# Hybrid attention encoder on one core: one wide buffer per chunk of keys, values or queries, and the copy of a group's sums moved behind the exponentials

## The chip, the cores and the metric

The kernel runs on one core of a Trainium2 chip. The core has TensorE (PE, the matrix engine), VectorE (DVE), ScalarE (ACT), GpSimd (POOL) and SyncE (SP), which here only issues transfers. Each engine works through its own instructions in order. The metric is the device time of one execution in microseconds (us); lower is better.

## The reference, cut to what matters

One encoder layer is computed for a prompt of 256 tokens and a sample of 2048 tokens, apart from each other:

```python
h    = rmsnorm(x, norm_pre)                       # 1024 wide
u, b, c, z_conv, q_lat, kv_lat, k_pe, z_attn = split(h @ w_in)
conv = b * short_conv(c * u, conv_w) * silu(z_conv)       # 3 taps, 512 wide
q    = rmsnorm(q_lat, q_norm) @ w_uq              # 384 -> 8 heads x (64 + 32)
kv   = rmsnorm(kv_lat, kv_norm) @ w_ukv           # 256 -> 8 heads x (64 keys + 64 values)
q    = [q_nope, rope(q_pe)];  k = [k_nope, rope(k_pe) for every head]
att  = softmax(q @ k.T / sqrt(96)) @ v * silu(z_attn)     # full, not causal
y    = x + rmsnorm([conv, att] @ w_out, norm_post)
```

Everything is float32. The kernel keeps that precision by splitting values into a high and a low part and multiplying the parts apart: three matmuls (lines 91 to 93) for one product.

## The kernel before

**Phase 1** (up to about 646 us) makes the combined projection. It leaves the latents, the gates and the convolution branch in DRAM.

**Phase 2** turns the latents into keys, values and queries, chunk by chunk. There are nine chunks of 256 tokens, one of the prompt and eight of the sample. Keys and values of all chunks come first (`keys`: four products `m`, each 128 rows by 256 tokens; `values`: two products of 128 tokens by 512), then the queries in the order 1, 2, 0, 3, ..., 8 (`queries`: six products; `m` 4 and 5, which come first, are the parts to be rotated, 0 to 3 the rest). A product takes its PSUM buffer from `bank`, which goes in a cycle of three: the first half of a wide buffer (128 x 1024), its second half, and a narrow buffer "o" (128 x 512). There are two wide and two narrow "o" buffers. The halves of a wide buffer are one tile for the program that places the waits, which has this visible effect in the trace: a matmul into the second half waits for the reads of the first.

Each product of keys or queries is read at once by `split` (line 71: ScalarE writes the high part `sk` or `sq`; line 72: VectorE the low part), or by `rope` (lines 578 to 581: VectorE a shuffle and a product, GpSimd a product and a sum). The rotated queries `sqr` are split into `sqp` at `m == 2`, and `sqp` is stored in DRAM there; `sq` is stored at `m == 3`. `sqr` and `sqp` exist once each, blocks `sk` and `sq` have three buffers together. SyncE's transfers stand in one queue, in an order that the scheduler of the language gives them; the order on TensorE, VectorE, ScalarE and GpSimd is that in which the program is written, from the first key block on.

Once the keys are in DRAM, the heads' keys are loaded (`k`, line 688 ff.), eight transfers that use the hardware's queue of SyncE, and the queries of block 0 after the chunks 1 and 2 (`load_q(0)`, line 714), since block 0 is 512 queries of the sample's first two chunks. From the third query chunk of the sample on, the generator `beside` goes on by two pieces for each query product: the first maxima of block 0 (`m`, line 751; VectorE's reduction `mx`, line 752; two narrow buffers "m"), then the prompt's whole attention.

**Phase 3, attention** (832 to 1531 us) has 16 groups, one for each pair of heads and block of 512 queries, with eight periods each. A period takes two tiles of 128 keys. Its score matmuls go into two wide buffers (`first`, line 788: two matmuls for each head and tile; `second`, line 793: one with the maxima). Between the first ones stand the maxima of a group to come, after the second ones the products with the values for the period before (line 917, into a narrow buffer "o"). Then ScalarE takes the two exponentials (line 798, 128 x 1024 each, into `p`) and GpSimd adds each `p` to the running sum `acc` (line 808). The sums of a group are used in the next one. `finish` begins there at the third period (`at == 2`): two matmuls add `acc` over the partitions (`r`, line 817, a buffer "m"), ScalarE copies `r` to `rsum` (line 819), VectorE takes four reciprocals (line 822), GpSimd multiplies the gate with them (line 824), VectorE multiplies the result with the gate (`res`, line 827) and frees the buffer "o" by it. Each call of `settle` goes one `yield` further, one call to a period, and in the period it stands ahead of the exponentials:

```python
self.settle()
for x, o in enumerate(os):
    s = 2 * p + x
    self.exponents(s, o)
    if at or x:
        self.total(n, ...)
```

While the groups 0 to 13 run, the output weights are cut in pieces by ScalarE and GpSimd (`spare`).

**Phase 4** multiplies 18 tiles of 128 tokens with the output weights, in the order 16, 17, 0, ..., 15. A tile is split as well: ScalarE writes the high part (line 942), GpSimd the low part (line 943), and the last eight of 24 matmuls for each half of the output (line 956) use the low part. The split of the first tile (16) is written after the last period.

Of the kernel before, what the change touches and what calls it, by code (L numbers as in the profile page):

```python
# [21 lines left out]
P = 128  # L22
# [37 lines left out]
def f(ap):  # L60
    return ap.bitcast(F32)
# [327 lines left out]
class Phase2:  # L389
# [169 lines left out]
    def run(self, pv):  # L559
# [3 lines left out]
        with ExitStack() as ctx:  # L563
            pb = ctx.enter_context(tc.tile_pool(name="p2b", bufs=2, reuse_waits="tile"))

            def bank(name):
                self.turn += 1
                if self.turn % 3 == 0:
                    return g.narrow(name, "o")
                if self.turn % 3 == 1:  # L570
                    self.pair = g.wide(name)
                half = self.turn % 3 - 1
                return self.pair[:, half * 512 : (half + 1) * 512]

# [14 lines left out]

            def keys(ci):  # L590
# [3 lines left out]
                hi, lo = ws["uk"]  # L594
                for m in range(4):
                    o = bank(f"k{ci}_{m}")[:, :n]
                    msl = slice(m * P, (m + 1) * P)
                    mm3(nc, o, [(hi[:, k, msl], lo[:, k, msl], lt[:, :, 0, k], lt[:, :, 1, k]) for k in range(2)])
                    split(nc, sk[:, 0, m], sk[:, 1, m], o, BACK)
                    if m == 3:  # L600
                        store(g.kn, sk, slice(at, at + n))
                    yield "k", ci, m

            def values(ci):
                at, n = self.chunks[ci]
                lt, _ = self.lt["kv", ci]
                hi, lo = ws["uv"]
                for m in range(n // P):
                    o = bank(f"v{ci}_{m}")
                    mm3(nc, o, [(lt[:, m, 0, k], lt[:, m, 1, k], hi[:, k, :], lo[:, k, :]) for k in range(2)])  # L610
                    nc.scalar.activation(pv[:, at // P + m], o, AF.Copy, scale=BACK)
                    yield "v", ci, m

            def queries(ci):
# [6 lines left out]
                hi, lo = ws["uq"]  # L621
                for m in (4, 5, 0, 1, 2, 3):
                    o = bank(f"q{ci}_{m}")[:, :n]
                    msl = slice(m * P, (m + 1) * P)
                    mm3(nc, o, [(hi[:, k, msl], lo[:, k, msl], lt[:, :, 0, k], lt[:, :, 1, k]) for k in range(3)])
# [524 lines left out]
```

## Time and profile before

| what | time |
| --- | --- |
| median of three runs | 1751.0 us (1750.26 to 1751.06) |
| the profiled execution | 1750.81 us |
| its span in the profile | 1748.9 us |
| TensorE busy (matmuls) | 1658.3 us, 95% |
| GpSimd busy | 859.4 us, 49% |
| VectorE busy | 757.9 us, 43% |
| ScalarE busy | 591.0 us, 34% |
| mean granted clock of TensorE | 0.990 |
| GpSimd's running sum `acc`, one of 224 | 2.354 us |
| GpSimd's product of gate and `rsum`, one of 16 | 1.27 us |

The span is the time between the first and the last instruction in the trace. TensorE is nearly always busy, so the pauses that remain on it, and the stretches in which its clock falls, are what a change of order can alter; a busy share of another engine tells only whether it could take more work. The granted clock is given as a share of full speed.

### The profile page before, as it was taken

The numbers are of one execution on the slowest core, as the hardware profiler recorded it, in microseconds if no ns is written. First come the engines' busy times: TensorE is split into PE (matmuls) and PEld (weight loads), VectorE is DVE, ScalarE is ACT, GpSimd is POOL, SyncE is SP. The second block draws the span as 40 slices with busy tenths as digits, with TensorE's granted clock in tenths as the row PEclk, the third lists the DMA queues.
The fourth block names the chain that finished last, engine by engine and source line by source line (L and its number), as shares of the span: only waits on it lengthen the run. The fifth ranks groups of instructions, "written<-read, shape, count | busy, mean of one in ns | idle before, by whom it ended". The sixth has DMA issues, their size and how long they took to land.

```text
span 1748.9 us, 22522 instructions
## 1 busy us (share of the span) xinstructions
PE 1658.3 (95%) x8870; PEld 1120.3 (64%) x8870; DVE 757.9 (43%) x1214; ACT 591.0 (34%) x867; POOL 859.4 (49%) x638
## 2 busy tenths in 40 slices
PE   8999999999999997787999999999999999989998
PEld 8999999999999984555333333333333333368886
DVE  4333332323663312365555555555655555122222
ACT  7521112452231123322444444444444444511111
POOL 3221221122522110123788888889888888942222
PEclk9999999999999999988999999999999999999999
DMA  8921112544342124646111131113111210034443
GB/s 285 284 75 49 58 51 88 147 122 122 102 141 81 64 75 119 169 140 162 38 30 31 43 85 36 43 31 91 30 43 31 67 43 13 13 108 144 139 133 114
DMA packets 141741, 158.97 MB, mean 91 GB/s; under 512 B 33842, under 2 KB 118116, under 8 KB 141636
## 3 DMA queue, kind: packets, MB, share of 16 engines
q1 hardware_dynamic: 141636, 157.55, 30.1%
q8 instruction: 69, 1.13, 0.3%
q14 instruction: 36, 0.29, 0.1%
HBM read 109.72 MB, written 41.89 MB: 87 GB/s over the span
## 4 chain that ended last, share of the span: by engine, by line
PE 48%; ACT 2%; DVE 2%; issue 1%; POOL 1%; POOLq 0%; ACTq 0%; DVEq 0%
PE o L917 13%; PE s L788 12%; PE out L954 7%; PE m L751 6%; PE out L956 4%; PE s L793 4%; POOL acc L808 1%; ACT p L798 1%; DVE mx L752 1%; PE r L817 1%; PE mr L775 1%; ACT rsum L819 1%; PE q L91 0%; PE q L93 0%; PE q L92 0%
## 5 line engine op out<-in xcount | busy, mean ns | idle before, releaser
L808 POOL TENSOR_TENSOR acc<-acc,p 128x1024 f32<-128x1024 f32 x224 | 527.3, 2354 | 81.7 <-ACT p L798 68.8
L752 DVE TENSOR_REDUCE mx<-m 128x1 f32<-128x512 f32 x512 | 338.6, 691 | 270.8 <-PE m L751 270.8
L798 ACT ACTIVATE p<-s,exps 128x1024 f32<-128x1024 f32 x256 | 271.3, 1112 | 300.3 <-PE s L793 295.9
L788 PE MATMUL s<-q,k 128*128 128x512 f16 x1024 | 301.5, 379 | 26.5 <-ACT p L798 26.5
L91 PE MATMUL o<-hdn_hi,whi 128*128 128x384 f32 x960 | 323.5, 337 | 0.0
L92 PE MATMUL o<-hdn_lo,whi 128*128 128x384 f32 x960 | 322.7, 336 | 0.0
L93 PE MATMUL o<-hdn_hi,wlo 128*128 128x384 f32 x960 | 322.6, 336 | 0.0
L917 PE MATMUL o<-p,v 128*64 128x512 f32 x1024 | 247.7, 605 | 0.0
L788 PEld LDWEIGHTS <-k 128*128 128x128 f16 x1024 | 91.7, 98 | 211.5 <-issue 120.6
L751 PE MATMUL m<-k,q 96*128 96x512 f16 x512 | 194.5, 381 | 2.3 <-DVE mx L752 1.5
L91 PEld LDWEIGHTS o<-hdn_hi,whi 128*128 128x128 f32 x960 | 180.5, 188 | 0.5
L92 PEld LDWEIGHTS o<-hdn_lo,whi 128*128 128x128 f32 x960 | 180.5, 188 | 0.0
L93 PEld LDWEIGHTS o<-hdn_hi,wlo 128*128 128x128 f32 x960 | 180.5, 188 | 0.0
L917 PEld LDWEIGHTS o<-p,v 128*64 128x64 f32 x1024 | 62.2, 136 | 127.5 <-issue 127.0
L954 PE MATMUL out<-wo,o_cut 128*128 128x512 f32 x576 | 140.4, 396 | 0.0
L954 PEld LDWEIGHTS out<-wo,o_cut 128*128 128x128 f32 x576 | 108.0, 188 | 27.6 <-ACT o_cut L942 0.8
L943 POOL TENSOR_TENSOR o_cut<-o_raw,o_cut 128x1024 fp32r<-128x1024 f32 x18 | 43.0, 2393 | 118.6 <-ACT o_cut L942 118.6
L236 ACT ACTIVATE whi<-w 128x1024 fp32r<-128x1024 f32 x40 | 42.2, 1058 | 172.0 <-PE o L92 157.8
L279 POOL TENSOR_TENSOR gt<-gt,z 128x384 f32<-128x384 f32 x24 | 29.4, 1224 | 142.0 <-ACT z L278 142.0
L962 DVE TENSOR_TENSOR yt<-out,g_post 128x1024 f32<-128x1024 f32 x18 | 22.1, 1225 | 163.6 <-ACT junko L961 163.6
L751 PEld LDWEIGHTS <-q 96*128 96x128 f16 x512 | 49.4, 96 | 59.3 <-issue 1.3
L271 POOL TENSOR_TENSOR cu<-cu,rb 128x384 f32<-128x384 f32 (+2 forms) x28 | 27.5, 987 | 112.5 <-DVE cu L270 112.5
(229 smaller groups left out, 2030.9 us busy)
## 6 DMA issues: line engine op xcount, KB each, us to landing
w<-in_w_e_dram SPq DMA_DIRECT2D x40, 512.0 KB, 3.4
x<-in_x_dram SPq DMA_DIRECT2D x18, 512.0 KB, 6.2
o_raw<-mix_s SPq DMA_DIRECT2D x18, 512.0 KB, 4.7
o_raw<-in_x_dram SPq DMA_DIRECT2D x18, 512.0 KB, 5.6
out_dram<-yt SPq DMA_DIRECT2D x18, 512.0 KB, 6.2
q<-qn_s SPq DMA_DIRECT2D x64, 128.0 KB, 2.8
xt<-in_x_t_dram SPq DMA_DIRECT2D x5, 1536.0 KB, 8.2
k<-kn_s SPq DMA_DIRECT2D x12, 512.0 KB, 6.2
```

The costliest lines, as they stand in the source:

```text
L91: nc.tensor.matmul(out, sh, mh, start=first and i == 0, stop=False)
L92: nc.tensor.matmul(out, sh, ml, start=False, stop=False)
L93: nc.tensor.matmul(out, sl, mh, start=False, stop=last and i == n - 1)
L751: nc.tensor.matmul(m, q[:DQK, i, 2, b * P : (b + 1) * P], k[:DQK, i, 1, c * 512 : (c + 1) * 512], start=True, stop=True)
L752: nc.vector.reduce_max(mx[:, u, c : c + 1], m, axis=AX.X)
L788: nc.tensor.matmul(o, k[:, ki, x, ks], q[:, qi, x, :], start=x == 0, stop=False)
L793: self.g.nc.tensor.matmul(o, self.kc[rows, ks], c[rows], start=False, stop=True)
L798: nc.scalar.activation(p, o, AF.Exp, scale=g.exps[:, 0:1])
L808: nc.gpsimd.tensor_tensor(self.acc[key], self.acc[key], first, op=ALU.add)
L917: nc.tensor.matmul(self.o[n][i * DV : (i + 1) * DV], g.v[:, kt, h * DV : (h + 1) * DV], p[:, i * QB : (i + 1) * QB], start=kt == 0, stop=k ...
L954: nc.tensor.matmul(o[:, w], mh[:, k, :], wk[k // 2][:, k % 2, w], start=k == 0 and wk is hi, stop=False)
L956: nc.tensor.matmul(o[:, w], ml[:, k, :], hi[k // 2][:, k % 2, w], start=False, stop=k == 7)
```

## The change

It has three edits. In phase 2, `bank` goes; the four products of a key chunk, the two of a value chunk and the four unrotated ones of a query chunk fill one wide buffer of their own (`wide`), and it is read once, when whole: one `split` over 1024 columns, or one copy. The two rotated products share one narrow buffer and one `rope` over 512 columns. The split and store of `sqp` stand after those of `sq`, at `m == 3`. In attention, `settle` stands behind the loop over the two exponentials and sums. In phase 4, the low part of the first tile (16) is made by VectorE instead of GpSimd.

```diff
@@ -563,21 +563,13 @@ Phase2.run
-            def bank(name):
-                self.turn += 1
-                if self.turn % 3 == 0:
-                    return g.narrow(name, "o")
-                if self.turn % 3 == 1:
-                    self.pair = g.wide(name)
-                half = self.turn % 3 - 1
-                return self.pair[:, half * 512 : (half + 1) * 512]
-
-            def rope(dst, src, tb, n, name):
-
-                t = pb.tile([P, CB], F32, tag="rs", bufs=2, name=f"rs_{name}")[:, :n]
+            def rope(dst, src, tb, name):
+
+                t = pb.tile([P, 2, CB], F32, tag="rs", bufs=2, name=f"rs_{name}")[:, :, : src.shape[2]]
+                cos, sin = (tb[:, w : w + 1, : src.shape[2]].to_broadcast(list(src.shape)) for w in range(2))
                 nc.vector.stream_shuffle(t, src, SWAP)
-                nc.vector.tensor_tensor(dst, src, tb[:, 0, :n], op=ALU.mult)
-                nc.gpsimd.tensor_tensor(t, t, tb[:, 1, :n], op=ALU.mult)
+                nc.vector.tensor_tensor(dst, src, cos, op=ALU.mult)
+                nc.gpsimd.tensor_tensor(t, t, sin, op=ALU.mult)
                 nc.gpsimd.tensor_tensor(dst, dst, t, op=ALU.add)
...
+            def wide(name, m, n):
+                return g.wide(name)[:, : m * n].rearrange("p (m t) -> p m t", m=m)
 
             def keys(ci):
...
+                o = wide(f"k{ci}", 4, n)
                 for m in range(4):
-                    o = bank(f"k{ci}_{m}")[:, :n]
                     msl = slice(m * P, (m + 1) * P)
...
-                    split(nc, sk[:, 0, m], sk[:, 1, m], o, BACK)
                     if m == 3:
+                        split(nc, sk[:, 0], sk[:, 1], o, BACK)
                         store(g.kn, sk, slice(at, at + n))
                     yield "k", ci, m
...
+                o = wide(f"v{ci}", n // P, H * DV)
                 for m in range(n // P):
-                    o = bank(f"v{ci}_{m}")
...
-                    nc.scalar.activation(pv[:, at // P + m], o, AF.Copy, scale=BACK)
+                    if m == n // P - 1:
+                        nc.scalar.activation(pv[:, at // P : (at + n) // P], o, AF.Copy, scale=BACK)
                     yield "v", ci, m
...
+                r = g.narrow(f"qr{ci}", "o")[:, : 2 * n].rearrange("p (m t) -> p m t", m=2)
+                o = wide(f"q{ci}", 4, n)
                 for m in (4, 5, 0, 1, 2, 3):
-                    o = bank(f"q{ci}_{m}")[:, :n]
                     msl = slice(m * P, (m + 1) * P)
...
-                    if m >= 4:
-                        rope(sqr[:, m - 4], o, tb, n, f"q{ci}_{m}")
-                    else:
-                        split(nc, sq[:, 0, m], sq[:, 1, m], o, BACK)
-                    if m == 2:
+                    if m == 5:
+                        rope(sqr, r, tb, f"q{ci}")
+                    if m == 3:
+                        split(nc, sq[:, 0], sq[:, 1], o, BACK)
+                        store(g.qn, sq, tok)
                         split(nc, sqp[:, 0], sqp[:, 1], sqr, BACK)
                         store(g.qr, sqp, tok)
-                    if m == 3:
-                        store(g.qn, sq, tok)
                     yield "q", ci, m
@@ -894,12 +889,12 @@ Attention.steps
-        self.settle()
         for x, o in enumerate(os):
             s = 2 * p + x
             self.exponents(s, o)
             if at or x:
                 self.total(n, self.p[s - 1] if not at else self.p[s], None if at else self.p[s])
+        self.settle()
@@ -940,7 +935,9 @@ Phase4.split
         m, _, mh, ml = self.ready[i]
         nc.scalar.activation(mh, m, AF.Copy)
-        nc.gpsimd.tensor_tensor(ml, m, f(mh), op=ALU.subtract)
+
+        eng = nc.vector if i == T // P - 2 else nc.gpsimd
+        eng.tensor_tensor(ml, m, f(mh), op=ALU.subtract)
```

ScalarE's order in attention, around the third period of the second group; `s` are score tiles, `p` their exponentials, `r` the partition sums. Before:

```order
L798 ACTIVATE p_7795<-s_7765,exps 128x1024
L798 ACTIVATE p_7797<-s_7766,exps 128x1024
L798 ACTIVATE p_7833<-s_7802,exps 128x1024
L798 ACTIVATE p_7836<-s_7803,exps 128x1024
L819 ACTIVATE rsum_7873<-r_7870 128x512
L798 ACTIVATE p_7875<-s_7840,exps 128x1024
L798 ACTIVATE p_7878<-s_7841,exps 128x1024
```

After (line numbers are those of the changed kernel, in which 793 is the exponential and 814 the copy):

```order
L793 ACTIVATE p_7635<-s_7604,exps 128x1024
L793 ACTIVATE p_7638<-s_7605,exps 128x1024
L793 ACTIVATE p_7672<-s_7642,exps 128x1024
L793 ACTIVATE p_7675<-s_7643,exps 128x1024
L814 ACTIVATE rsum_7681<-r_7678 128x512
L793 ACTIVATE p_7713<-s_7683,exps 128x1024
L793 ACTIVATE p_7716<-s_7684,exps 128x1024
```

The copy has moved from ahead of the third period's two exponentials to behind them.

GpSimd's order at the end of the same `finish`, in the group's seventh period; `gate` is the product of line 824 before, 819 after, all others are running sums. Before:

```order
L808 TENSOR_TENSOR acc_7799<-acc_7799,p_7986 128x1024
L808 TENSOR_TENSOR acc_7799<-acc_7799,p_7989 128x1024
L824 TENSOR_TENSOR gate_7427<-gate_7427,rsum_7873 128x512
L808 TENSOR_TENSOR acc_7799<-acc_7799,p_8027 128x1024
L808 TENSOR_TENSOR acc_7799<-acc_7799,p_8030 128x1024
L808 TENSOR_TENSOR acc_7799<-acc_7799,p_8079 128x1024
```

After:

```order
L803 TENSOR_TENSOR acc_7601<-acc_7601,p_7787 128x1024
L803 TENSOR_TENSOR acc_7601<-acc_7601,p_7790 128x1024
L803 TENSOR_TENSOR acc_7601<-acc_7601,p_7827 128x1024
L803 TENSOR_TENSOR acc_7601<-acc_7601,p_7830 128x1024
L819 TENSOR_TENSOR gate_7229<-gate_7229,rsum_7681 128x512
L803 TENSOR_TENSOR acc_7601<-acc_7601,p_7878 128x1024
```

The product with the gate stands two sums later than it did against the exponentials' tiles: it was ahead of the seventh period's sums, and is now behind them.

VectorE's order in the first query chunk of phase 2: the rotation (a shuffle and a product), the splits `sq`, and the split `sqp` of the rotated part. Before:

```order
L578 STREAM_SHUFFLE rs_q_4_6290<-q_4_6280 128x256
L579 TENSOR_TENSOR sqr_6277<-q_4_6280,tb_6147 128x256
L578 STREAM_SHUFFLE rs_q_5_6304<-q_4_6280 128x256
L579 TENSOR_TENSOR sqr_6277<-q_4_6280,tb_6147 128x256
L72 SCALAR_TENSOR_TENSOR sq_6279<-q_0_6309,sq_6279 128x256
L72 SCALAR_TENSOR_TENSOR sq_6279<-q_1_6321,sq_6279 128x256 x2
L72 SCALAR_TENSOR_TENSOR sqp_6278<-sqr_6277,sqp_6278 128x512
L72 SCALAR_TENSOR_TENSOR sq_6279<-q_3_6347,sq_6279 128x256
```

After:

```order
L570 STREAM_SHUFFLE rs_q_6219<-qr_6199 128x512
L571 TENSOR_TENSOR sqr_6196<-qr_6199,tb_6084 128x512
L72 SCALAR_TENSOR_TENSOR sq_6198<-q_6200,sq_6198 128x1024
L72 SCALAR_TENSOR_TENSOR sqp_6197<-sqr_6196,sqp_6197 128x512
L570 STREAM_SHUFFLE rs_q_6294<-qr_6274 128x512
```

Six instructions on products of 256 columns and one of 512 have become two of 512 and one of 1024, and `sqp` stands after the whole of `sq`; the last row is the next chunk's.

VectorE's order where attention ends and the output begins; the two `res` are the results of groups 13 and 14, between them stand the reciprocals of group 14, and `yt` is the first tile of the output. Before:

```order
L822 RECIPROCAL rsum_12211<-rsum_12211 128x128
L827 TENSOR_TENSOR res_12401<-o_11843,gate_11778 128x512
L822 RECIPROCAL rsum_12482<-rsum_12482 128x128 x4
L827 TENSOR_TENSOR res_12611<-o_12167,gate_12103 128x512
L962 TENSOR_TENSOR yt_12692<-out_12636,g_post 128x1024
```

After, with the subtraction of the first tile (line 940):

```order
L822 TENSOR_TENSOR res_12209<-o_11645,gate_11580 128x512
L817 RECIPROCAL rsum_12290<-rsum_12290 128x128 x4
L822 TENSOR_TENSOR res_12419<-o_11969,gate_11905 128x512
L940 TENSOR_TENSOR o_cut_1_12424<-o_raw_12422,o_cut_0_12423 128x1024
L959 TENSOR_TENSOR yt_12494<-out_12438,g_post 128x1024
```

The subtraction stands between the result of group 14 and the first tile's output.

## Rows read from the trace of the kernel before

**Rows 1.** Whom TensorE waits for, whole span: us in total, times, longest us.

```profile
PE s L788 <- ACT p L798: 26.5, 16, 1.7
```

**Rows 2.** The same view, 744 to 832 us.

```profile
PE q L91 <- DVE sqr L579: 5.9, 5, 2.9
...
PE q L91 <- DVE sq L72: 2.4, 4, 0.9
```

**Rows 3.** Windows: length, busy of PE, PEld, DVE, ACT, POOL; clock, DMA share, GB/s.

```profile
744.00:832.00 88.00, 72.02 (x484) 45.93 (x483) 54.09 (x120) 22.25 (x48) 25.29 (x32) 0.88 0.55 150
832.00:1528.00 696.00, 668.37 (x3208) 224.29 (x3207) 388.15 (x586) 303.81 (x317) 596.00 (x271) 1.00 0.15 42
```

**Rows 4.** TensorE, 690 to 700: start, duration, operation, idle time before and what ended it.

```profile
691.20 0.27 PE L91 MATMUL k<-lt_kv,uk_hi 128*128 128x256 f16 x1
691.31 0.27 PE L92 MATMUL k<-lt_kv,uk_hi 128*128 128x256 f16 x1
...
696.06 0.38 PE L91 MATMUL k<-uv_hi,lt_kv 128*128 128x512 f16 x1 [0.93 <-DVE sk L72]
...
698.65 0.27 PE L91 MATMUL k<-lt_kv,uk_hi 128*128 128x256 f16 x1
```

**Rows 5.** VectorE's groups by form: busy us, mean ns, idle before.

```profile
L964 DVE SCALAR_TENSOR_TENSOR yt<-yt,sqo,o_raw 128x1024 f32<-128x1024 f32 x18 | 23.1, 1285 | 1.6
...
L72 DVE SCALAR_TENSOR_TENSOR sk<-k,sk 128x256 f16<-128x256 f32 x36 | 15.3, 425 | 48.8 <-ACT sk L71 48.8
```

**Rows 6.** SyncE's issues, 710 to 745.

```profile
714.12 0.63 SPq L692 DMA_DIRECT2D k<-kn_s  x1
...
726.60 0.55 SPq L585 DMA_DIRECT2D qr_s<-sqp  x1
...
733.92 0.37 SPq L585 DMA_DIRECT2D qr_s<-sqp  x1
...
736.40 0.32 SPq L714 DMA_DIRECT2D q<-qr_s  x1
```

**Rows 7.** ScalarE, 728 to 736.

```profile
732.54 0.63 ACT L71 ACTIVATE sqp<-sqr 128x512 f16<-128x512 f32 x1 [3.41 <-DMA qr_s<-sqp]
```

**Rows 8.** TensorE, 713 to 744.

```profile
713.53 0.27 PE L91 MATMUL q<-lt_q,uq_hi 128*128 128x256 f16 x1
...
734.96 0.37 PE L91 MATMUL q<-lt_q,uq_hi 128*128 128x256 f16 x1 [4.28 <-DVE sqr L579]
...
743.53 0.60 PE L751 MATMUL m<-k,q 96*128 96x512 f16 x2
```

**Rows 9.** All engines, a group's third period, 930 to 941.

```profile
934.01 1.03 PE L817 MATMUL r<-acc,ones_f 128*64 128x512 f32 x4
...
935.08 0.60 ACT L819 ACTIVATE rsum<-r 128x512 f32<-128x512 f32 x1 [5.88 <-PE r L817]
935.58 2.12 ACT L798 ACTIVATE p<-s,exps 128x1024 f32<-128x1024 f32 x2
936.74 0.59 PE L788 MATMUL s<-q,k 128*128 128x512 f16 x2 [1.70 <-ACT p L798]
```

**Rows 10.** All engines, the end of a gate's way, 911 to 920.

```profile
911.08 2.12 ACT L798 ACTIVATE p<-s,exps 128x1024 f32<-128x1024 f32 x2 [3.00 <-PE s L793]
...
917.07 0.68 DVE L827 TENSOR_TENSOR res<-o,gate 128x512 f32<-128x512 f32 x1
...
919.62 0.69 DVE L752 TENSOR_REDUCE mx<-m 128x1 f32<-128x512 f32 x1 [1.87 <-PE m L751]
```

**Rows 11.** All engines, from attention to the output, 1526 to 1556.

```profile
1528.67 9.73 POOL L808 TENSOR_TENSOR acc<-acc,p 128x1024 f32<-128x1024 f32 x4
...
1531.04 4.00 PE L954 MATMUL out<-wo,o_cut 128*128 128x512 f32 x16
...
1540.75 3.52 PE L956 MATMUL out<-wo,o_cut 128*128 128x512 f32 x8 [5.71 <-POOL o_cut L943]
```

**Rows 12.** One line's instructions: count, shortest/median/longest ns, first and last start, form.

```profile
L237 DVE TENSOR_TENSOR wlo<-w,whi x40: 1202/1226/1806, 54.5 to 622.0; 128x1024 fp32r<-128x1024 f32 x40
```

More of the change, by code (lines that the diff above doesn't have):

```diff
@@ L594, in keys @@
                 hi, lo = ws["uk"]
+                o = wide(f"k{ci}", 4, n)
                 for m in range(4):
-                    o = bank(f"k{ci}_{m}")[:, :n]
                     msl = slice(m * P, (m + 1) * P)
-                    mm3(nc, o, [(hi[:, k, msl], lo[:, k, msl], lt[:, :, 0, k], lt[:, :, 1, k]) for k in range(2)])
-                    split(nc, sk[:, 0, m], sk[:, 1, m], o, BACK)
+                    mm3(nc, o[:, m], [(hi[:, k, msl], lo[:, k, msl], lt[:, :, 0, k], lt[:, :, 1, k]) for k in range(2)])
                     if m == 3:
+                        split(nc, sk[:, 0], sk[:, 1], o, BACK)
                         store(g.kn, sk, slice(at, at + n))
@@ L607, in values @@
                 hi, lo = ws["uv"]
+                o = wide(f"v{ci}", n // P, H * DV)
                 for m in range(n // P):
-                    o = bank(f"v{ci}_{m}")
-                    mm3(nc, o, [(lt[:, m, 0, k], lt[:, m, 1, k], hi[:, k, :], lo[:, k, :]) for k in range(2)])
-                    nc.scalar.activation(pv[:, at // P + m], o, AF.Copy, scale=BACK)
+                    mm3(nc, o[:, m], [(lt[:, m, 0, k], lt[:, m, 1, k], hi[:, k, :], lo[:, k, :]) for k in range(2)])
+                    if m == n // P - 1:
+                        nc.scalar.activation(pv[:, at // P : (at + n) // P], o, AF.Copy, scale=BACK)
                     yield "v", ci, m
@@ L621, in queries @@
                 hi, lo = ws["uq"]
+                r = g.narrow(f"qr{ci}", "o")[:, : 2 * n].rearrange("p (m t) -> p m t", m=2)
+                o = wide(f"q{ci}", 4, n)
                 for m in (4, 5, 0, 1, 2, 3):
-                    o = bank(f"q{ci}_{m}")[:, :n]
                     msl = slice(m * P, (m + 1) * P)
-                    mm3(nc, o, [(hi[:, k, msl], lo[:, k, msl], lt[:, :, 0, k], lt[:, :, 1, k]) for k in range(3)])
-                    if m >= 4:
-                        rope(sqr[:, m - 4], o, tb, n, f"q{ci}_{m}")
-                    else:
-                        split(nc, sq[:, 0, m], sq[:, 1, m], o, BACK)
-                    if m == 2:
+                    mm3(nc, o[:, m] if m < 4 else r[:, m - 4], [(hi[:, k, msl], lo[:, k, msl], lt[:, :, 0, k], lt[:, :, 1, k]) for k in range(3)])
+                    if m == 5:
[3 more added lines that the diff above has]
+                        store(g.qn, sq, tok)
                         split(nc, sqp[:, 0], sqp[:, 1], sqr, BACK)
                         store(g.qr, sqp, tok)
-                    if m == 3:
-                        store(g.qn, sq, tok)
                     yield "q", ci, m
```

## The prediction

> **What bounds the kernel now.** I read the busy shares first, then who TensorE waits for, and then the three stretches that the change touches. TensorE is busy for 1658 us of a span of 1748.9 us, so time can only come out of its pauses and out of what they do to its clock. The list of its waits [rows 1] puts the largest total, 26.5 us in 16 pauses of at most 1.7 us, on score matmuls (line 788) that wait for an exponential. Next come pauses of the key matmuls behind VectorE's piece of a split, 18 in all (one is the 0.93 us in [rows 4]), and those of the query matmuls, of which the later chunks hold 5.9 and 2.4 us [rows 2]. The windows [rows 3] show the difference between the two stretches: during attention (832 to 1528) the granted clock is 1.00 and TensorE works 668 of 696 us, with GpSimd at 596; between 744 and 832 it works 72 of 88 us at a mean clock of 0.88. The last pause is the tail's, 5.71 us behind GpSimd [rows 11].
>
> **Part 1, keys and values.** Now a chunk takes 7.45 us (691.20 to 698.65 in [rows 4]). Its 24 key matmuls follow each other every 0.11 us and its 12 value matmuls every 0.215, which is 2.6 + 2.6 = 5.2 us of issue. The rest is two pauses: the two halves of a wide buffer count as one tile, so the second half's matmuls wait until ScalarE and VectorE have read the first. In the change nothing reads a buffer before it is whole, and keys and values take the two wide buffers in turn. The next keys need the buffer that the last keys left 2.6 us of values ago; ScalarE's piece over 1024 columns costs about 1.06 us (half of the 2.12 in [rows 9]) and VectorE's about 1.29 [rows 5], with some 0.35 us of latencies: 2.7 us, so about 0.1 us stays open. The value buffer has only a ScalarE copy and is free long before. So 5.3 us a chunk, 2.15 saved, nine chunks: 19.4 us. Bounds: no pause gives 20. If VectorE's long piece costs four short ones (4 x 0.425 = 1.70 [rows 5]), 0.4 us more stays open in each: 16. Below nothing is excluded, since the same matmuls lose two pauses.
>
> **Part 2, the first three query chunks.** Here the matmuls gain but the start of the next work does not. The first maxima (743.53 in [rows 8]) need the loaded queries of block 0, and these need the rotated parts of the second chunk in DRAM. Their buffer `sqp` exists once: ScalarE begins the second chunk's only when the first chunk's store has landed, 732.54 after a wait of 3.41 us [rows 7]. That store was issued at 726.60 [rows 6] and took 5.9 us, because the key loads were in front of it, eight transfers that begin at 714.12. From the first key load to that landing it is 18.4 us. In the change the last keys' store goes out about 2.6 us later against the first query matmul, since the last VectorE piece now ends with the values; the store of `sqp` stands behind that of `sq` (512 KB), for which I add 1.2 us. Then come ScalarE 0.63, VectorE 0.7, the store to the next load 2.5 us (733.92 to 736.40, [rows 6]), two more issues that wait for nothing new, and a landing that I take as another 2.5. With T for the first query matmul: first key load T + 3.3, landing T + 22.9, rotated parts stored T + 24.4, maxima at T + 29.5. Today it is T + 30.0 (713.5 to 743.53). TensorE itself would be there at T + 18.7: three chunks of 54 matmuls at 0.11 us and nine more. So the four short pauses and the one of 4.28 us [rows 8] become one pause of about 10.8 us, and I count 0.5 us of gain. Bounds: 11 if the loads don't hold it, and a loss of 3 if each of the two stores lands 1.7 us later than I take.
>
> **Part 3, chunks 4 to 9 of the queries, beside the maxima and the prompt.** Five pauses behind the rotation (5.9 us) and four behind a split (2.4 us) go [rows 2], since a second piece no longer shares a tile that is being read. The clock's half-speed time after the longest, 2.9 us, should go as well; I count 3 us for that out of the 0.12 x 88 = 10.6 us that the stretch loses to the clock [rows 3]. Against it: at the end of a chunk VectorE now waits for one long ScalarE piece (1.06), then works 1.29 + 0.69 us on the splits while two buffers of maxima fill. Where a chunk ends in two maxima (the first one) TensorE reaches the third after 1.4 us and VectorE has freed its buffer after 4.0: 2.5 us lost. At the first score tiles the second one takes the buffer of the last queries: 1.5 us, and 0.5 for the third maximum. Sum -8.3 - 3 + 2.5 + 2 = -6.8. Bounds: -11 (nothing new waits) and +5 (each of six chunk ends costs 2.5, and no clock comes back).
>
> **Part 4, the copy of the sums.** In 15 of the 16 pauses TensorE's row is that of [rows 9]: `r` ends at 935.05, the copy waits for it until 935.08 with the engine idle for 5.88 us, and both exponentials, whose scores were there three microseconds earlier, come after it; the next score matmul waits 1.70 us for the first of them. In the change the exponentials start some 3 us earlier and are over before `r` is. The copy then starts at the same time as now, so the bank of `r`, which the second maximum needs a microsecond later, is free no later. That is 15 x 1.7 = 25.5 us. On GpSimd the product with the gate moves behind two sums of about 2.35 us. VectorE's `res` waits for it. Today `res` starts at 917.07 and the next reduction at 919.62 [rows 10]: the gate then would end about 5.2 us after the period's second exponential (913.20, two sums and the product of 1.27 us in the table of times), 918.4, `res` 919.1. That fits before 919.62. In the groups in which GpSimd also cuts the output weights it runs 1 to 2 us later, and the reductions slip: I charge 2 us over all groups. Net -23.5. Bounds -25.5 and -17 (0.6 us in every group).
>
> **Part 5, the tail.** GpSimd's last four sums begin at 1528.67, and the second part of the first output tile stands behind them: TensorE starts at 1531.04, pauses 5.71 us and then runs eight matmuls in 3.52 us instead of 1.87 [rows 11]. On VectorE the subtraction follows `res` of group 14, which now waits for a gate behind two of these four sums: about 1533.2, `res` 0.7, subtraction 1.23 [rows 12], ready at 1535.2 where TensorE wants it at 1534.8. A pause of 0.4 us keeps the clock: 5.3 + 1.65 = 7 us gained. Bounds 7.4 and 2.5.
>
> The same subtraction form took 1.20 to 1.81 us, 1.23 in the middle [rows 12]. [...] The spread of that row agrees with some contention, and by it 1.23 would become 1.8, or 3.6 if a whole sum is waited out.
>
> **Sum.** 19.4 + 0.5 + 6.8 + 23.5 + 7 = 57.2 us. The profiled execution took 1750.81 us, 1.9 more than its span and 0.2 under the median of 1751.0; 1750.8 - 57.2 = 1693.6, so I say 1694.
>
> **Rivals.**
> - Loads do not set the start of the maxima (part 2 gains its 11): 1683. For it: the stores may go out earlier than today's order of the queue. Against: the 3.41 us wait on the single buffer. 0.10.
> - The wide pieces hold VectorE (part 1 at 16, part 3 at +5): 1694 + 3.4 + 11.8 = 1709. For it: 54 of 88 us busy on VectorE with TensorE's maxima behind it [rows 3]. Against: the same work in fewer instructions. 0.17.
> - The subtraction in the tail waits out a GpSimd sum: ready 3.0 us later, and the half clock's 1.65 us comes back: 1699. 0.07.
> - The copy's move does nothing, because something else holds the score tiles' buffers: 1694 + 23.5 = 1717. Against it: ScalarE idle for 5.88 us before the copy. 0.05.
> - Slower: GpSimd becomes the bound of attention. Its 596 us fit into the 671 that are left, but `res` and so the reductions would hang on its lag. From a lag of about 4.5 us in each of 14 groups this costs over 4 us a group and eats all 57: 1755. Against: GpSimd now idles before the third period's sums, which is the time that comes forward. 0.04.
>
> **How the numbers follow.** The forecast holds 0.57; its own range by the nearer bounds is 1688 to 1702. For 8 in 10 I reach part of the way to the first two rivals: 1685 to 1708. No change can be told within 0.2%, 3.5 us; only the last rival ends there or above: faster 0.95, same 0.01, slower 0.04.
>
> **What would show it.** Part 1: a chunk of keys and values every 5.3 us. Part 2: one pause of 8 to 13 us before the first maximum, ScalarE's second `sqp` still waiting for a store. Part 3: no wait behind the rotation, new ones of a microsecond or two behind maxima. Part 4: the 26.5 us of line 788 behind exponentials under 3, `rsum` behind both exponentials, GpSimd's idle time before the third period about halved. Part 5: less than 1 us between the 16th and the 17th output matmul. Wrong would be: reductions that start late in most groups, a granted clock below 0.85 from 720 to 810, or key chunks that wait for their loaded latents.

## The result, and the profile after

The changed kernel takes 1692.53 us (median of four runs, 1691.07 to 1694.51) against 1750.63 us for the kernel before (four runs, 1747.6 to 1751.06). The ratio is 0.9672, with a 95% interval of 0.9656 to 0.9689. The forecast was 1694, with a range of 1685 to 1708.

TensorE is busy for 1650 of 1692 us. Its list of waits, which answers to [rows 1, 2] (us in total, times, the longest):

```profile
PE m L746 <- DMA q<-qr_s: 8.9, 1, 8.9
...
PE m L746 <- DVE mx L747: 4.6, 6, 1.2
...
PE m_p L736 <- DMA q_p<-qr_s: 2.1, 1, 2.1
...
PE s L783 <- DVE sq L72: 1.1, 1, 1.1
PE s L783 <- ACT p L793: 1.0, 1, 1.0
```

The score matmuls' 26.5 us behind exponentials have become one pause of 1.0 us. The pauses of the key matmuls and those behind the rotation are gone. New at the top is a single one of 8.9 us, in front of the first maxima; in the third row, the prompt's first maxima wait 2.1 us for its queries. The windows that answer to [rows 3] (columns as there) show that attention still runs at full clock (1.00) and that phase 2's end still does not (0.90):

```profile
722.00:802.00 80.00, 68.98 (x478) 45.41 (x479) 50.37 (x84) 17.87 (x28) 22.98 (x20) 0.90 0.60 164
803.00:1477.00 674.00, 668.93 (x3205) 223.52 (x3205) 392.11 (x586) 305.62 (x318) 595.49 (x271) 1.00 0.16 44
```

The table has the lengths of five stretches, each from the first start of one instruction to that of the next in the trace of a kernel. Their ends are the first key matmul, the first query matmul, the first maximum, the first exponential of attention's second group, the first output matmul, and the span's end.

| stretch, us | before | after | gained | forecast gain |
| --- | --- | --- | --- | --- |
| keys and values | 66.83 | 46.89 | 19.9 | 19.4 |
| first three query chunks | 30.00 | 29.42 | 0.6 | 0.5 |
| rest of phase 2 and group 0 | 134.23 | 129.68 | 4.5 | 6.8 |
| groups 1 to 15 | 653.28 | 628.26 | 25.0 | 23.5 |
| output | 217.82 | 211.92 | 5.9 | 7 |

With 0.4 us of phase 1, which the change does not touch, this is, but for rounding, the 56.5 us between the spans 1748.9 and 1692.4. The third stretch as a window, before and after (columns as in [rows 3]):

```profile
743.53:877.76 134.23, 116.67 (x697) 61.05 (x694) 81.64 (x165) 41.66 (x68) 59.61 (x47) 0.92 0.42 115
722.58:852.26 129.68, 115.99 (x695) 61.42 (x695) 78.55 (x128) 38.58 (x50) 57.29 (x35) 0.93 0.45 122
```

The first column behind the length is TensorE's busy time: it is idle for 17.6 us before and 13.7 after, and busy for 0.7 us less.

**Keys and values.** TensorE's timeline that answers to [rows 4]: keys, values and the next keys follow one another without a bracket, that is without idle time, 5.21 us a chunk.

```profile
672.32 0.27 PE L91 MATMUL k<-lt_kv,uk_hi 128*128 128x256 f16 x1
...
674.94 0.38 PE L91 MATMUL v<-uv_hi,lt_kv 128*128 128x512 f16 x1
...
677.53 0.27 PE L91 MATMUL k<-lt_kv,uk_hi 128*128 128x256 f16 x1
```

**The first maxima.** TensorE's timeline from the first query matmul to the first maximum, for [rows 8]:

```profile
693.16 0.27 PE L91 MATMUL qr<-lt_q,uq_hi 128*128 128x256 f16 x1
...
712.20 0.27 PE L91 MATMUL qr<-lt_q,uq_hi 128*128 128x256 f16 x1 [1.18 <-DMA lt_q<-lat_s]
...
722.58 1.01 PE L746 MATMUL m<-k,q 96*128 96x512 f16 x2 [8.90 <-DMA q<-qr_s]
```

SyncE's issues in this time, for [rows 6]: the first key load, the two stores of `sqp`, and the first load of rotated queries:

```profile
696.28 0.62 SPq L687 DMA_DIRECT2D k<-kn_s  x1
...
708.10 2.64 SPq L577 DMA_DIRECT2D qr_s<-sqp  x1
...
716.88 0.36 SPq L577 DMA_DIRECT2D qr_s<-sqp  x1
...
720.05 0.54 SPq L709 DMA_DIRECT2D q<-qr_s  x1
```

ScalarE's second `sqp`, for [rows 7]:

```profile
715.50 0.63 ACT L71 ACTIVATE sqp<-sqr 128x512 f16<-128x512 f32 x1 [9.32 <-DMA qr_s<-sqp]
```

From the first query matmul (693.16) it is 3.1 us to the first key load, 22.3 to ScalarE's second `sqp`, which waits 9.32 us for the first one's store, and 29.4 to the first maximum. The forecast had 3.3, 22.9 and 29.5. TensorE spends the time in one pause of 8.90 us, and in one of 1.18 us for the latents of the fourth chunk; the forecast had a single one of about 10.8.

**Attention.** All engines in the third period of the third group, for [rows 9]:

```profile
904.92 2.12 ACT L793 ACTIVATE p<-s,exps 128x1024 f32<-128x1024 f32 x2 [3.00 <-PE s L788]
...
906.73 1.03 PE L812 MATMUL r<-acc,ones_f 128*64 128x512 f32 x4
...
907.69 0.60 PE L783 MATMUL s<-q,k 128*128 128x512 f16 x2
907.80 0.60 ACT L814 ACTIVATE rsum<-r 128x512 f32<-128x512 f32 x1 [0.77 <-PE r L812]
```

The exponentials are done at 907.04, before `r` is (907.76); the copy starts right after it and keeps nobody from the score tiles.

**The tail.** All engines, for [rows 11]:

```profile
1480.52 4.01 PE L951 MATMUL out<-wo,o_cut 128*128 128x512 f32 x16
...
1482.18 5.75 POOL L803 TENSOR_TENSOR acc<-acc,p 128x1024 f32<-128x1024 f32 x2
...
1482.87 2.80 DVE L940 TENSOR_TENSOR o_cut<-o_raw,o_cut 128x1024 fp32r<-128x1024 f32 x1
...
1485.72 2.13 PE L953 MATMUL out<-wo,o_cut 128*128 128x512 f32 x8 [1.20 <-DVE o_cut L940]
```

VectorE begins the subtraction at 1482.87, but it takes 2.80 us; TensorE pauses 1.20 us instead of 5.71, and its next eight matmuls take 2.13 us at a granted clock of 1.00 (0.57 for those in [rows 11]).

### The profile page after: what moved, and what is told of

The parts are those of the page before. It is cut to its first block, busy times and chain, and to the rows that moved or that the text cites. A ratio compares the mean times of both kernels' runs of the same rounds, so it can differ in the third digit from the quotient of the medians.

```text
span 1692.4 us, 22351 instructions
## 1 busy us (share of the span) xinstructions
PE 1650.2 (98%) x8870; PEld 1117.6 (66%) x8870; DVE 753.8 (45%) x1134; ACT 581.2 (34%) x804; POOL 854.3 (50%) x619
```

## The experiments

Twelve runs. Each gives the edit against the named kernel, what was expected, and what came. "Against the changed kernel" is judged by spans and stretches of profiled executions, because single runs of one kernel differ by some 3 us.

**Each edit alone.** The first three runs carry one edit of the diff each, on the kernel before: phase 2, `settle`, the tail.

> Phase 2 with its wide buffers alone; attention and the tail as before. The three edits act in three stretches, so their gains should add: a chunk of keys and values every 5.21 us (19.9 us in all), about 0.6 us on the first three query chunks, 6.5 us on the rest of phase 2 (with the slow clock at the start of attention taken off): 27 us, a time near 1723.5 us. The pauses of the score matmuls behind exponentials stay at 26 us in all. Rival (the edits feed each other): attention, which starts earlier, also changes its period of 44.2 us, and the time is under 1720 or over 1728.

> The move of settle alone, on the kernel before. By the prediction's part 4 the period of a group falls from 44.2 to 42.45 us, and the 15 pauses of 1.70 us go: 24 to 25 us, a time near 1726 us. The tail's pause behind GpSimd stays between 4 and 7 us. Rival (the gain in attention needs phase 2's other buffers as well): less than 20 us, over 1731.

> The subtraction of the first output tile on VectorE alone, on the kernel before. There the gate of group 14 still stands ahead of GpSimd's two sums, so VectorE is free when ScalarE's part is done. Theory (two pressures: the subtraction is lengthened by GpSimd's sums beside it, but starts in time): it takes 2.4 to 2.9 us, TensorE's pause in front of the 17th output matmul is under 0.3 us, gain 7.4 us, 1743.2. Rival (the subtraction is long for another reason, its late start): 1.2 to 1.3 us here, with the same time. Second rival (no gain, since the later GpSimd splits become late): over 1749.

Measured on one chip beside the kernel before (1748.86 us): phase 2 alone 1726.34 us, ratio 0.987 (0.9854 to 0.9885); `settle` alone 1723.98, ratio 0.9859 (0.9846 to 0.9873); the tail alone 1741.04, ratio 0.9956 (0.9944 to 0.9969). That is 22.5 + 24.9 + 7.8 = 55.2 us. All three together, timed again later beside the kernel before (1749.42), took 1694.28 us, which is 55.1 us less. So within the 2 or 3 us by which single runs differ the edits do not feed each other, and the rivals that said so fall. The stretches agree. Phase 2 alone has 46.89, 29.51 and 129.68 us in the first three rows of the table and 653.21 in attention; `settle` alone has 628.28 us in attention, and the tail's pause stays at 4.8 us. Phase 2 alone gained less than the 27 us expected: its first three stretches are 24.9 us shorter than in the profiled kernel before, but the third of them takes 131.89 and 132.17 us in the two runs that leave phase 2 as it was, and 134.23 in that profile.

In the tail-only kernel the subtraction starts in time, and TensorE does not pause at all; all engines there:

```profile
1528.96 1.62 DVE L945 TENSOR_TENSOR o_cut<-o_raw,o_cut 128x1024 fp32r<-128x1024 f32 x1 [1.07 <-ACT o_cut L942]
...
1529.49 3.99 PE L956 MATMUL out<-wo,o_cut 128*128 128x512 f32 x16
...
1533.32 2.03 PE L958 MATMUL out<-wo,o_cut 128*128 128x512 f32 x8
```

It took 1.62 us, neither the 2.4 to 2.9 that I expected nor the rival's 1.2 to 1.3. The experiment on the last sums comes back to this.

**Small pieces that share no tile.** On the kernel before:

```diff
             def bank(name):
                 self.turn += 1
-                if self.turn % 3 == 0:
+                if self.turn % 2 == 0:
                     return g.narrow(name, "o")
-                if self.turn % 3 == 1:
-                    self.pair = g.wide(name)
-                half = self.turn % 3 - 1
-                return self.pair[:, half * 512 : (half + 1) * 512]
+                return g.wide(name)[:, :512]
```

> The kernel before with its small pieces, but no product shares a tile with another: the products alternate between a wide buffer, of which the first half alone is used, and a narrow one. Theory (the shared tile makes the second half's matmuls wait): the 18 pauses of the key matmuls behind VectorE and the long ones behind the rotation go although the pieces are as small and as many as before; a chunk of keys and values takes 5.2 to 5.4 us; 20 to 30 us gained, 1721 to 1731. Rival (small pieces are too slow for VectorE and ScalarE, and the wide piece is what helps): a chunk stays above 6.5 us and less than 10 us are gained, over 1740.

1719.45 us, ratio 0.9838 (0.9824 to 0.9851): 29.4 us faster than before and 6.9 us faster than phase 2 with its wide buffers. VectorE's group of splits of keys, by form:

```profile
L72 DVE SCALAR_TENSOR_TENSOR sk<-k,sk 128x256 f16<-128x256 f32 x36 | 15.3, 425 | 30.0 <-ACT sk L71 30.0
```

TensorE's waits there; no key matmul waits for `sk` any more, and what waits for the rotation is 0.4 us:

```profile
PE s L785 <- ACT p L795: 26.5, 16, 1.7
PE q L91 <- DVE sq L72: 7.1, 2, 6.3
...
PE q L91 <- DVE sqr L576: 0.4, 1, 0.4
```

VectorE has the same 36 pieces of 425 ns as in [rows 5], and keys and values take 46.89 us as in the wide kernel. So the shared tile was the cause, not the size of the pieces. The long pause that is left, 6.3 us behind `sq`, belongs to the wait before the first maxima: ScalarE's second `sqp` waits 8.09 us for the first one's store there, and VectorE's `sqp` and `sq` stand behind it.

The wide piece is even the worse choice here. Of the 6.9 us, 1.5 lie in the first three query chunks and 5.0 in the third stretch. That stretch as a window, phase 2 alone and then the unshared kernel:

```profile
722.75:852.43 129.68, 114.48 (x695) 60.77 (x695) 78.49 (x128) 38.58 (x50) 57.29 (x35) 0.94 0.45 122
721.05:845.76 124.71, 110.47 (x695) 58.53 (x695) 80.48 (x161) 41.69 (x69) 58.84 (x47) 0.97 0.47 127
```

TensorE is idle about as long (15.2 and 14.2 us), but its 695 matmuls are busy for 4.0 us longer with the wide pieces, at a mean granted clock of 0.94 against 0.97. One place of this is the start of attention. TensorE's timeline there in the changed kernel:

```profile
805.08 0.59 PE L783 MATMUL s<-q,k 128*128 128x512 f16 x2 [1.07 <-DVE sq L72]
806.28 0.38 PE L746 MATMUL m<-k,q 96*128 96x512 f16 x1 [0.60 <-DVE mx L747]
...
809.38 0.99 PE L783 MATMUL s<-q,k 128*128 128x512 f16 x2 [0.99 <-ACT p L793]
```

Two windows of the same place, the last but two column being the granted clock:

```profile
803.00:809.40 6.40, 3.56 (x17) 1.18 (x16) 4.83 (x7) 2.47 (x4) 0.00 (x0) 1.00 0.56 140
809.40:812.80 3.40, 3.40 (x9) 1.21 (x9) 1.37 (x2) 0.93 (x1) 2.34 (x1) 0.51 1.02 245
```

The second score tile waits 1.07 us for the last wide split, the next maximum 0.60 us, and after the third pause (0.99, which the kernel before has too, with a granted clock of 1.00 behind it) the granted clock is 0.51 for 3.4 us, which by the share that is missing costs 3.4 x 0.49 = 1.7 us: 1.07 + 0.60 + 1.7 = 3.4 us. The unshared kernel has only the 0.99 there, at 1.00. But these pauses do not settle the clock: in the changed kernel timed again they are the same (1.07, 0.61 and 0.99), and the window that answers to the second one is at 1.00.

```profile
808.60:812.00 3.40, 3.25 (x15) 1.27 (x16) 2.54 (x4) 0.97 (x1) 2.35 (x1) 1.00 1.00 243
```

In the copy-only run the pauses are 1.1 and 1.0 us for the wide split and the exponential, and the matmuls of the whole stretch are busy for 113.13 us, where the profile of the changed kernel has 115.99 and that of the same kernel timed again 113.19. So the 1.67 us of waiting are shown as a cost of the wide pieces. Why the clock was lower with them in the rest of the stretch is not shown; the two kernels differ in the order of two stores as well.

**The copy alone behind the exponentials.** On the changed kernel, `settle` goes behind the loop in the third period only:

```diff
+        if at != 2:
+            self.settle()
         for x, o in enumerate(os):
...
-        self.settle()
+        if at == 2:
+            self.settle()
```

> The changed kernel, but only the first step of a group's finish (the partition sums and their copy) stands behind the exponentials; the later ones (reciprocals, gate, result) stand ahead of them as in the kernel before. Theory (the copy alone gives the gain in attention, and the gate behind two sums is a pure cost): the two pauses of 0.75 us behind reductions, in groups 5 and 12, go; all groups take 42.4 us; the subtraction of the first output tile begins when ScalarE's part is done, so the tail's pause of 1.2 us goes. 2 + 1.2 us, a span near 1689.2 us against 1692.4. Rival (GpSimd's cutting of the output weights makes those groups late wherever the gate stands): both pauses stay, span over 1691.

1690.88 us, ratio 0.9672 (0.9656 to 0.9688); span 1686.7. Groups 1 to 15 take 626.44 us instead of 628.26 and the output 210.48 instead of 211.92, so 3.3 us are gained as expected; 2.2 us more of this execution's span lie in the rest of phase 2 and group 0, where the matmuls are busy for 113.13 us and not 115.99. In the changed kernel the start of group 5 (the first group is 0) shows what the gate's place cost, by all engines:

```profile
1018.84 1.26 POOL L819 TENSOR_TENSOR gate<-gate,rsum 128x512 f32<-128x512 f32 x1
...
1020.14 0.69 DVE L822 TENSOR_TENSOR res<-o,gate 128x512 f32<-128x512 f32 x1 [2.93 <-POOL gate L819]
...
1020.74 2.49 DVE L747 TENSOR_REDUCE mx<-m 128x1 f32<-128x512 f32 x4
...
1021.48 0.38 PE L746 MATMUL m<-k,q 96*128 96x512 f16 x1 [0.75 <-DVE mx L747]
```

GpSimd, late by two cuts of the output weights (1.27 us each, at 1006.89 and 1012.86), ends the gate at 1020.1; VectorE's `res` has waited 2.93 us for it, the reductions behind it are late, and the next maximum waits 0.75 us. It is so in group 12 as well, and nowhere else; with the gate ahead of the sums neither pause is there. The rival falls.

**What holds the first maxima.** Two runs on the changed kernel: the prompt's key loads asked for after block 0's queries, and two buffers for `sqp`.

```diff
             at.load_k(0)
-            at.load_k("p")
...
             at.load_q(0)
+            at.load_k("p")
```

```diff
-                sqp = pb.tile([P, 2, 2, CB], F16, tag="sqp", bufs=1, ...
+                sqp = pb.tile([P, 2, 2, CB], F16, tag="sqp", bufs=2, ...
```

> The changed kernel, with the prompt's key loads asked for after the loads of block 0's queries; four of their five transfers then stand behind the latter in SyncE's queue (the first one still ahead). Theory of part 2 (the key loads in front delay the stores of the rotated queries, and these the first maxima): the first maximum comes 3 to 6 us earlier than the 29.4 us after the first query matmul, TensorE's pause of 8.9 us shrinks to 3 to 6 us; the prompt's first maxima may wait longer than 2.1 us for their keys. Rival (the stores take their time whatever is in front): first maximum within 1 us of 29.4 us.

> The changed kernel with two buffers for the split of the rotated queries. If the single buffer alone holds the first maxima (part 2's chain as predicted), ScalarE's wait of 9.3 us for a store goes and the first maximum comes 2 us or more earlier than 29.4 us after the first query matmul. Rival, now the likelier: the store of the unrotated queries of the same chunk lands as late (718.67) as the rotated ones (719.41), because both stand behind the key loads in the queue; the wait of ScalarE goes, the first maximum moves by less than 1.5 us.

With two buffers (1693.21 us, one run) ScalarE's wait of 9.32 us is gone, and the first maximum comes 28.8 us after the first query matmul instead of 29.4. With the loads moved it comes after 24.3 us, 5.1 earlier. So the transfers in front of the stores hold the start, and the single buffer hardly does. But moving them gained nothing in the whole: 1693.34 us, ratio 0.9684 (0.967 to 0.9698). The 5.1 us are lost again one stage later, as TensorE's waits in the run with the loads moved show:

```profile
PE m L746 <- DMA q<-qr_s: 5.4, 1, 5.4
...
PE m_p L736 <- DVE mx L747: 5.0, 1, 5.0
```

**Where those 5 us went.** The prompt's first maxima wait 5.04 us. Two more runs on the kernel with the loads moved: first with 20 instead of 12 of block 0's maxima ahead of the prompt's, then with two buffers for `sqp` as well (the edit above).

```diff
         for i, _ in enumerate(first):
             yield
-            if i == 11:
+            if i == 19:
                 break
```

> The run with late prompt keys again, with 20 instead of 12 of block 0's maxima ahead of the prompt's. There the first maxima came 5.1 us earlier, and all of it was lost again at the prompt's first maxima, which waited 5.04 us. Theory (they wait for the prompt's queries, which stand in SyncE's queue behind a latent load that waits for its buffer): with eight more maxima in front, the pause shrinks to under 1 us and attention starts 3 to 5 us earlier: a span of 1687 to 1689 us. Rival (the stretch is bound by VectorE's reductions, so any order takes as long): a span over 1691.

> The run before last (late prompt keys, 20 maxima ahead of the prompt) with two buffers for the split of the rotated queries. The theory on the prompt's queries fell: TensorE paused at the same place, 733.64, for 4.72 us. New theory: ScalarE's split of the next rotated queries waits 3.10 us for the store that empties the single buffer, VectorE's share of that split waits for ScalarE's, and the reductions stand behind it in VectorE's order. With two buffers ScalarE's wait goes and TensorE's pause there shrinks to under 1 us. Rival (the reductions are late for VectorE's own work): the pause stays above 3 us. The span stays over 1690, since the later prompt costs at other places.

The first took 1700.03 us, ratio 0.9722 (0.9709 to 0.9736), and paused at 733.64 again, for 4.72 us, though no prompt query was wanted there. My theory fell. ScalarE's next split of rotated queries in that run (in the run before it is the same, at 731.36 with a wait of 3.11 us):

```profile
731.64 0.63 ACT L71 ACTIVATE sqp<-sqr 128x512 f16<-128x512 f32 x1 [3.10 <-DMA qr_s<-sqp]
```

VectorE's share of it and the reductions behind:

```profile
732.30 0.69 DVE L72 SCALAR_TENSOR_TENSOR sqp<-sqr,sqp 128x512 f16<-128x512 f32 x1 [2.50 <-ACT sqp L71]
732.91 2.65 DVE L747 TENSOR_REDUCE mx<-m 128x1 f32<-128x512 f32 x4
```

With two buffers as well (1699.2 us, one run) ScalarE's wait is gone, and TensorE's pause there is 2.07 us: most of it was the single buffer, but not down to the 1 us I had expected. Both runs are slower as a whole. From the first maximum to the second group they take 141.48 and 140.07 us, where the changed kernel takes 129.68, at a mean granted clock of 0.89 and 0.87 against 0.93. By length times the share of the clock that is missing, as the prediction reckons it, 15.6 and 18.2 us are lost to the clock against 9.1, so by this estimate 6.5 and 9.1 of the 11.8 and 10.4 us are lost to the lower clock. I put that down to the prompt's work, which comes later, but have not tested it. So the single buffer, which does not hold the first maxima, holds the reductions once the loads are out of the way. What an order would gain that serves both stayed untried.

**The last sums on VectorE.** On the changed kernel; `late` is set for the last two periods.

```diff
         else:
-            nc.gpsimd.tensor_tensor(self.acc[key], self.acc[key], first, op=ALU.add)
+            eng = nc.vector if late else nc.gpsimd
+            eng.tensor_tensor(self.acc[key], self.acc[key], first, op=ALU.add)
```

> The changed kernel, with the last four running sums on VectorE instead of GpSimd, so that GpSimd is idle beside the subtraction of the first output tile. Theory (contention with GpSimd's sums made it 2.80 us long): 1.2 to 1.3 us, TensorE's pause of 1.2 us goes. Rival (the form itself is slow there, right behind the result): 2.4 us or more.

1694.64 us (one run): the subtraction took 2.81 us again, TensorE paused 1.72. GpSimd was not idle as I had meant it to be: it had the gate and then the next tile's split. GpSimd's timeline at this place, the next tile's split:

```profile
1481.64 3.07 POOL L941 TENSOR_TENSOR o_cut<-o_raw,o_cut 128x1024 fp32r<-128x1024 f32 x1 [0.27 <-ACT o_cut L938]
```

VectorE's timeline, the subtraction:

```profile
1482.98 2.81 DVE L941 TENSOR_TENSOR o_cut<-o_raw,o_cut 128x1024 fp32r<-128x1024 f32 x1
```

GpSimd's instruction ends at 1481.64 + 3.07 = 1484.71, the subtraction at 1485.79, 1.08 us later. The same in the changed kernel, beside the subtraction of 1482.87 above; GpSimd's timeline in a window that holds the sum in front alone:

```profile
1482.18 2.40 POOL L803 TENSOR_TENSOR acc<-acc,p 128x1024 f32<-128x1024 f32 x1
```

The same for the next sum:

```profile
1484.66 3.27 POOL L803 TENSOR_TENSOR acc<-acc,p 128x1024 f32<-128x1024 f32 x1
```

The sum in front ends at 1484.58, the subtraction at 1485.66 or 1485.67, again 1.08 later; the next sum, begun at 1484.66, takes 3.27 us instead of 2.40. In the tail-only kernel the sum in front ends at 1529.50 and the subtraction at 1530.58; in the copy-only kernel 1476.09 and 1477.17; in the last kernel below 1473.73 and 1474.82. In five of five VectorE's instruction, which began later, ends 1.08 or 1.09 us after GpSimd's, whatever it takes itself (1.48 to 2.81 us). For the last kernel the 1.08 us were expected before it ran (1.5 to 1.7 us in all; 1.48 came). The experiment did not take GpSimd's work away from beside the subtraction, but the rows show what its length goes with: the end of GpSimd's instruction in front.

**The parts put together.** The kernel before with unshared small pieces, the copy alone behind the exponentials, and the tail's subtraction on VectorE; beside it the changed kernel unaltered.

> The kernel before with three edits that the runs so far point to: small products that share no tile (as in the run with unshared buffers), only the partition sums and their copy behind the exponentials, and the subtraction of the first output tile on VectorE. If the gains add, the span is 1717.2 (unshared alone) less 24.9 and 1.9 in attention less 7.4 in the tail, 1683.0 us; a measured time near 1685, 0.4% under the changed kernel. VectorE's subtraction: it ends 1.08 us after the GpSimd instruction in front of it, 1.5 to 1.7 us in all. Rival (the start of attention loses its gain, as the clock falls elsewhere): span over 1687.

> The changed kernel unaltered, beside the others on one chip: 1691 to 1694 us.

1685.31 us, ratio 0.9641 (0.9627 to 0.9655), against 1694.28 us, ratio 0.9686 (0.9673 to 0.9699), on the same chip. Its span is 1684.3, with 46.89, 28.15, 125.44, 626.47 and 210.46 us in the five stretches. The gains add (29.4 of the unshared buffers, 24.9 and 1.8 in attention, 7.8 in the tail are 63.9 us; 64.1 came); it is the fastest of all, and it does without the wide buffers.

## Why the prediction was right

- **Keys and values**: right in mechanism and size (19.4 forecast, 19.9 measured, the upper bound was 20). The forecast 0.1 us that would stay open in each chunk does not show: ScalarE's and VectorE's wide pieces took 1.02 and 1.22 us, not 1.06 and 1.29. That the shared tile was the cause is shown by the unshared kernel.
- **First three query chunks**: the size was right (0.5 and 0.6) and the chain came as worked out, to within 0.7 us at each of its marks. Its cause was half wrong. I gave the single buffer `sqp` as a link of the chain; without it the first maximum moves by only 0.6 us, because block 0's loads wait for stores that land as late: in that run the second chunk's `sq` landed at 718.30, and the first load was issued at 718.31. The key loads in front of the stores set the time. (The kernel before has five short pauses beside the one of 4.28 us, not four; nothing in the sum hangs on it.) My rival in which the loads don't set it has fallen.
- **Rest of phase 2**: the pauses went in sum as forecast, but 4.5 us came instead of 6.8. TensorE's idle time fell by 3.9 us (17.6 to 13.7), where -8.3 + 2.5 + 2 gives 3.8. The step "I count 3 us" for the clock was mis-sized: the matmuls (697 and 695 in the trace) were busy for only 0.7 us less. At the start of attention 1.7 us were lost at a granted clock of 0.51 behind the two pauses forecast there (1.5 and 0.5; 1.07 and 0.60 measured), but not in the changed kernel timed again, which had the same pauses with the clock at 1.00. The 2.5 us at the first chunk's end did not come; two pauses of 1.2 us behind reductions in later chunks did. Busy time scatters by some 3 us between kernels with the same order there (before: 116.67, and 113.84 with `settle` alone, 114.11 with the tail alone; after: 115.99, 114.48 with phase 2 alone, 113.19 timed again, 113.13 copy-only). So a gain by the clock can't be told from these runs, and a miss of 2 us is within what the executions differ.
- **The copy**: right. 15 pauses of 1.70 us went, and the charge of 2 us for the gate behind two sums was 1.8 (the copy-only run gets it back), in two groups and not over all. 25.0 us against 23.5, since the whole gain is 626.44 against 653.28, 26.8, a little over 25.5.
- **The tail**: right in direction, 5.9 instead of 7. The step "subtraction 1.23" failed: it took 2.80, and TensorE's pause of 1.20 us missed the sign set for it (under 1 us). The rival in which the subtraction waits out a GpSimd sum fits the rows: 1.08 us from the sum's end to the subtraction's. It was priced at 3.0 us, though 3.6 less 1.23 is 2.4, and 1.65 for the clock; it cost 1.57, as the sum in front had already run for 0.7 us, and behind TensorE's pause of 1.20 us the clock was 1.00. Two readings were off and nearly cancel: by [rows 11] TensorE wants the low part at 1535.04 (1540.75 less 5.71), not at 1534.8, and eight matmuls that follow without a pause take 2.03 us in the tail-only kernel, not 1.87. It does not decide the total.
- **The slower rival** (GpSimd's lag) did not come. `res` does wait for the gate in every group, 1.2 us or more, where the first 13 waited for nothing before; but only in two groups did a late reduction hold TensorE, for 0.75 us each.

The profiled execution took 1694.51 us, the sum gave 1693.6: two terms that were too small by 0.5 and 1.5 us met two that were too large by 2.3 and 1.1, so part of the nearness is luck.

## What to carry to other kernels

If TensorE waits for the reads of one half of a buffer to write the other, give each product a buffer of its own before making the pieces larger: the small pieces gained more here (29.4 against 22.5 us). At the start of attention the next stage waited 1.67 us for the wide piece; the rest of the difference is not traced to a cause. Put in front of a shared engine's queue what another engine is waiting for (here both exponentials ahead of a copy), and move only that step: the rest of the chain that moved with it cost 3.3 us. Here the loads taken out of the way of the stores brought the first maximum 5.1 us earlier, and a wait of 5.04 us came one stage later (with 20 maxima ahead of the prompt it was 4.72 us with one buffer for the split, 2.07 with two), so look at the stretch, not at the wait.

## What the hardware showed that I had not expected

In these traces VectorE's subtraction and the GpSimd instruction beside it read as if they took turns. The subtraction took 1.48 (in two kernels), 1.62, 2.80 and 2.81 us, and ended 1.08 or 1.09 us after GpSimd's instruction in front in every one; GpSimd's next sum then took 3.27 us in the changed kernel and 3.26 in the copy-only one, where the kernel before has 2.354. The trace shows each of these lengths as busy time.

The trace of the kernel before had it already, in the spread of [rows 12]. GpSimd's timeline in a window that holds one instruction:

```profile
102.08 1.01 POOL L271 TENSOR_TENSOR cu<-cu,rb 128x384 f32<-128x384 f32 x1 [3.15 <-DVE cu L270]
```

VectorE's timeline, one of the 40 of that row:

```profile
102.36 1.80 DVE L237 TENSOR_TENSOR wlo<-w,whi 128x1024 fp32r<-128x1024 f32 x1 [0.36 <-ACT whi L236]
```

It ends at 104.16, 1.07 us after GpSimd's (103.09). All seven of the 40 that took over 1.26 us end 1.07 to 1.09 us after a GpSimd instruction that began before them. In three more GpSimd's had begun first as well, but VectorE took 1.20 to 1.23 us and GpSimd's was the long one (3.65, 1.97 and 2.44 us), so the starts alone do not say which of the two gets longer. What decides it is not shown.

The prediction named 1.8 us by the spread and 3.6 for a whole sum, and its sum went by 1.23. Read as turns, and with the sum's 2.354 us, my estimate is that a place behind a sum that has just begun costs up to 2.4 us, and a place right before its end almost nothing. Against 1.23 us, 0.25 (1.48) to 1.58 us (2.81) were measured.
